# A transformer block kernel: gate and readout pages issued from Pool's queue instead of SyncE's, and gate products spaced out at first

## The chip, the cores and the metric

The kernel runs on one core of a Trainium2 chip. The time is device microseconds of one execution, from the first to the last instruction and what lies around them; the figure given is the median of three executions. The profile is of one further execution, with its own time.

## The reference, cut to what matters

The block computes, for 512 latent tokens of width 2048 (and 256 context tokens that only set the starting state of a recurrence): modulation of the normalised input, one projection to 2048 channels, then two token mixers side by side, a pooling over four window sizes and a complex diagonal state-space scan ("S5") in both directions; an output projection; a gated residual; then a gated feed-forward of width 5632 with a 3x3 depthwise convolution, and a second gated residual.

```python
mx = jnp.split(s_c @ w_ada[l] + b_ada[l], 6, axis=-1)
u_lat = h_lat @ w_in[l]
hl = s5_scan(lat_g, lam_re, lam_im, bb_re, bb_im, h0, rev)
lat_dirs.append(s5_readout(hl, ssm_c_re[l, d], ssm_c_im[l, d]))
mix_lat = mix_project(u_lat, lat_dirs[0] + lat_dirs[1], w_pool[l], pool_scale[l], ssm_d[l], w_glu[l], w_out[l])
x = x + mx[2][:, None, :] * rms_norm(mix_lat, g_post_mix[l])
f_lat = conv_glu_ffn(modulate(rms_norm(x, g_pre_ffn[l]), mx[3], mx[4]), w_up[l], w_conv[l], w_down[l], rows)
x = x + mx[5][:, None, :] * rms_norm(f_lat, g_post_ffn[l])
```

Two of the six parts of `mx` are needed at once and are made by TensorE. The other four (called gates below: `mx[2]`, `mx[3]`, `mx[4]`, `mx[5]`) are needed only later; they are matrix-vector products that VectorE makes in the background, page by page.

## The kernel before, in words

**Weights.** All weights come in pages of 128 x 1024 fp32 (512 KB). `Stream` holds them in the order of use: `load` issues a page's transfer on SyncE's queue (L60, tile `raw`, two buffers), `make` splits it into a high part on ScalarE (L77, `whi`) and a low part on VectorE (L78, `wlo`), and `get` hands both to the caller, making one page ahead. Each product of matrices is three matmuls (`mm3`, L176 to L178: high by high, high by low, low by high), so a page is 24 matmuls of 512 columns.

**Foreground and background.** The foreground is the stream of weight pages: 24 pages of the input projection (`u_block`, tile `ub`), 8 of the pooling weights, 24 of the output projection (`wout_block`, tile `wo`) with the two pages of the gated unit among them (`glu`), 8 more of the output projection for the state-space channels (tile `wq`, weights `wbh` and `wbl`), then the feed-forward's pages (tiles `uh`, `up`, `dn`). Everything else is a generator in `Threads`: at each `tick` the foreground gives the generators a budget (the tick's nominal microseconds times a share: 0.76, later 0.84 and 0.95; one weight page counts 5.2), and they are stepped in order of priority. Each `yield c, lag` charges c to the budget and puts the next step at least `lag` weight pages later. The order in which the program is written out is the order of each engine's queue, and every engine works its queue in order.

**The generators that matter here.** `front` (priority 0) brings the state-space input into place (`UT`, products `bp`), adds `scan` (priority 2, on VectorE), copies the states out (`SN`), and runs the readout. `gemv` (priority 3) makes the gate products: each step issues the transfer of the page after next into the two-buffer tile `gv` (`gvload`, L172, on SyncE's queue) and then multiplies a page on VectorE (L972, `scr<-gv,srow`), at a charge of 1.4 and no lag. There are 82 such products. The gated unit, late in the output projection, needs the first 32 of the 96 gate pages (14 of them are multiplied earlier, outside `gemv`), and the transposes of `norm_pair` need all (`bg.finish(gv_t)`, L1137).

**The readout** runs in eleven rounds of one weight page each. `cl_build(u)` loads `cu` and `du` on SyncE's queue (L790, L792) and makes `cl` with four Pool operations and two on VectorE (L793 to L805). `window` copies `cl` into `R` on ScalarE (L812 to L814), `eb_mm` multiplies, `e_out` brings the result to DRAM on ScalarE's queue (L827 to L829, tensor `e_scratch`), and a round later `mi_load` reads it back in another shape (L834, tile `Mi`, 256 KB) on SyncE's queue, where it waits until the write has landed; `y_mm` uses it a round later still. Round u writes out, in this order: `eb_mm(u)`, `mi_load(u-1)`, `y_mm(u-2)`, then `window(u+1)`, `e_out(u)`, `cl_build(u+2)`.

Pool makes `mi` in the early part (`mi_build`, L562 to L564), `cl` in the readout, and later multiplies by the gate rows in `gate_piece` (L1088) and subtracts in `norm_pair` (L1159). Between the last `mi_build` and the readout it has no instruction but the clearings of `R`.

Of the kernel before, what the change touches and what calls it, by code (L numbers as in the profile page):

```python
# [129 lines left out]
def emit(tc, A, out, xs_dram, dbg=None):  # L130
    nc = tc.nc
    V, S, PO, PE = nc.vector, nc.scalar, nc.gpsimd, nc.tensor
# [7 lines left out]
    e_dram = nc.dram_tensor("e_scratch", (8, 32, 960), F32, kind="Internal").ap()  # L140
# [19 lines left out]
    def pg(name, shape=(1024,), dt=F32, parts=128):  # L160
        return shaped(sb.tile([128, 1024], dt, name=name, tag="pg", bufs=NPG), shape, slice(0, parts))

    def bank(name, cols=512, parts=128):
        t = ps.tile([128, 512], F32, name=name, tag="bank")
        return t[:parts, :cols]
# [1 line left out]
    def cst(name, shape, dt=F32):  # L167
        return sb.tile(shape, dt, name=name, tag=name)

    def gvload(ap, q=None):  # L170
        r = ring.tile([128, 1024], F32, name="gv", tag="gv", bufs=2)
        nc.sync.dma_start(r[:], ap)  # L172
        return r

    def mm3(o, ahi, alo, bhi, blo, start, stop):
# [391 lines left out]
    def mi_build(k, t, tmp):  # L567
        g0 = 4 * k
        m = t.rearrange("p (r g i h) -> p r g i h", r=2, g=4, i=8)
        for _ in cmul_build(m[:, 0], m[:, 1], BB[:, 0, g0:g0 + 4, :], BB[:, 1, g0:g0 + 4, :], PIN, g0, 4, PO, tmp):  # L570
            pass
        return m
# [4 lines left out]
    def mt_half(k, r):  # L577
        if r == 0:
            mts[k] = pg(f"mt{k}", (2, 4, 128))
        tp = bank("mtp")  # L580
        for g in range(4):
            PE.transpose(tp[:, g * 128:(g + 1) * 128], mis[k][:, r, g].rearrange("p i h -> p (i h)"), ident[:])
        S.activation(mts[k][:, r], tp.rearrange("p (g c) -> p g c", g=4), AF.Copy)
# [96 lines left out]
    def front():  # L680
        def mi_next(k):
            if k < 8:
                cm = pb.tile([128, 512], F32, name="cm", tag="cm", bufs=1)
                mis[k] = mi_build(k, pb.tile([128, 1024], F32, name="mi", tag="mi", bufs=1)[:], cm[:])

        for gb in range(4):
# [5 lines left out]
                                        ap=[[768, 8], [6144, 16], [1, 768]]), uc.rearrange("p i c -> p (i c)"))  # L692
        mi_next(NMT)
        yield 0.0, 1.0
        for gb in range(4):
            u = pg(f"UT{gb}", (8, NCH))
            UT[gb] = u
            nc.sync.dma_start(u, bass.AP(tensor=u_dram.tensor, offset=gb * 128 * 768,
                                         ap=[[96, 8], [6144, 16], [768, 8], [1, 96]]))
            yield 0.0, 0.5 if gb < 3 else 0.75  # L700
        for gb in range(4):
            for kk in range(2):
                k = 2 * gb + kk
                g0 = 4 * k
                if k >= NMT:
                    for r in range(2):
                        mt_half(k, r)
                    mi_next(k + 1)
                    yield 0.0, 0.4
                mt = mts.pop(k)  # L710
                for r in range(2):
                    bp = bank("bp", 4 * NCH)
                    for g in range(4):
                        PE.matmul(bp[:, g * NCH:(g + 1) * NCH], mt[:, r, g, :], UT[gb][:, (g0 + g) % 8, :],
                                  start=True, stop=True)
                    bv = bp.rearrange("p (g c) -> p c g", g=4)
                    dst = B[:, :, r, g0:g0 + 4]
                    S.activation(dst[0:64], bv[0:64], AF.Copy)
                    S.activation(dst[64:128, 0:32][:, ::-1], bv[64:128, 0:32], AF.Copy)
                    S.activation(dst[64:128, 32:96][:, ::-1], bv[64:128, 32:96], AF.Copy)  # L720
                yield 0.0, 1.6 if k == NMT else 0.3
# [65 lines left out]
        def cl_build(u):  # L787
            g4 = slice(4 * u, 4 * u + 4)
            cu = pc.tile([128, 2, 4, 16], F32, name="cu", tag="cu", bufs=3)
            nc.sync.dma_start(cu[:], A["ssm_c"][:, :, g4, :])  # L790
            du = pc.tile([128, 16], F32, name="du", tag="du", bufs=3)
            nc.sync.dma_start(du[:], A["ssm_d"][u])  # L792
            PO.tensor_tensor(du[:], du[:], hmask[:], op=OP.mult)  # L793
            cl = [pc.tile([128, 4, 8, 16], F32, name=f"cl{r}", tag=f"cl{r}", bufs=4)[:] for r in range(2)]
            ts = [p1.tile([128, 528], F32, name="cm", tag="ps2", bufs=2)[:, :512].rearrange(
                "p (g s h) -> p g s h", g=4, s=8) for _ in range(2)]
            sh = [128, 4, 8, 16]
            pr, pi = [POUT[:, :, r, g4].rearrange("p s g -> p g s").unsqueeze(3).to_broadcast(sh) for r in range(2)]
            xr, xi = [cu[:, r].unsqueeze(2).to_broadcast(sh) for r in range(2)]
            V.tensor_tensor(ts[0], xi, pi, op=OP.mult)  # L800
            PO.tensor_tensor(cl[0], xr, pr, op=OP.mult)
            V.tensor_tensor(ts[1], xi, pr, op=OP.mult)
            PO.tensor_tensor(cl[1], xr, pi, op=OP.mult)
            PO.tensor_tensor(cl[0], cl[0], ts[0], op=OP.subtract)
            PO.tensor_tensor(cl[1], cl[1], ts[1], op=OP.add)  # L805
            cls[u] = (cl, cu, du)
# [9 lines left out]
        def eb_mm(u):  # L816

            ebs[u] = eb = bank("eb", 240)
            for r in range(2):
                for g in range(4):  # L820
                    c = 512 * r + 16 * (4 * u + g)
                    PE.matmul(eb[32 * g:32 * g + 32], BBt[:, c:c + 32], R[r][:, g].rearrange("p m h -> p (m h)"),
                              start=(r == 0), stop=(r == 1))
# [7 lines left out]

        def mi_load(u):
            Mis[u] = mi = pc.tile([128, 4, 8, 16], F32, name="Mi", tag="Mi", bufs=2)
            nc.sync.dma_start(mi[:].rearrange("p g j h -> p g (j h)"),  # L834
                              bass.AP(tensor=e_dram.tensor, offset=u * 32 * 960,
                                      ap=[[16, 8], [960, 16], [240, 4], [1, 128]]))

        ebs = {}
        cl_build(0)
        cl_build(1)  # L840
        yield 2.8, 2.0
# [3 lines left out]
        for u in range(11):  # L845
            if u < 8:
                eb_mm(u)
            if 1 <= u <= 8:
                mi_load(u - 1)
            if 2 <= u <= 9:  # L850
                y_mm(u - 2)
            if u >= 4 and u % 2 == 0:
                yt_mm(u // 2 - 2)
            yield 0.0, 0.5
            if u < 7:
                window(u + 1)
            if u < 8:
                e_out(u)
            if 2 <= u <= 9:
                y_act(u - 2)  # L860
            if u >= 4 and u % 2 == 0:
                yt_act(u // 2 - 2)
            if u + 2 < 8:
                cl_build(u + 2)
            yield 1.4, 0.5

    yT, yTr = [None] * 2, [None] * 4
# [95 lines left out]
    def gemv():  # L963
        todo = [(c, n, hf) for c in range(3) for n in range(16) for hf in range(2)][2 * NGP:]
        tiles = []
        for x in range(len(todo)):

            while len(tiles) < min(x + 2, len(todo)):
                c, nt, hf = todo[len(tiles)]
                tiles.append(gvload(A["ada_n"][c, nt, hf]))  # L970
            c, nt, hf = todo[x]
            V.scalar_tensor_tensor(scr[:], tiles[x][:], 1.0, srow[:, hf * 1024:(hf + 1) * 1024], op0=OP.mult,  # L972
                                   op1=OP.mult, accum_out=gacc[:, hf, c, nt:nt + 1])
            tiles[x] = None
            gv_state[0] = 2 * NGP + x + 1
            if nt == 15 and hf == 1:
                gfin(c)
            yield 1.4, 0

    def gfin(c):  # L980
        a = acol[:, c, :]
# [123 lines left out]
    def norm_pair(rep):  # L1105
# [33 lines left out]
        for kk in range(8):  # L1139
# [21 lines left out]
            yield 1.8 * (kk % 2), 0  # L1161

    fr_t = bg.add(front(), 0)
    gv_t = bg.add(gemv(), 3)
    pb_t = []
    phs = {}
# [75 lines left out]

    frow = [pg(f"frow{j}", (2, 512)) for j in range(2)]

    def gemv5():
        for hf in range(2):
            sr = p2.tile([128, 1024], F32, name="srow2", tag="srow2", bufs=1)
            nc.sync.dma_start(sr[:], A["c_row"][:, hf * 1024:(hf + 1) * 1024])
            S.activation(sr[:], sr[:], AF.Silu)
            for nt in range(16):  # L1250
                r = gvload(A["ada_n"][3, nt, hf])
                yield 0.0, 1
                V.scalar_tensor_tensor(scr[:], r[:], 1.0, sr[:], op0=OP.mult, op1=OP.mult,
                                       accum_out=gacc[:, hf, 3, nt:nt + 1])
                yield 1.2, 0
        gfin(3)
        yield from rows_of(3, frow, p2, "srow2", 1)
# [134 lines left out]
    r = None  # L1392
    for t in range(4):
        os = {d: bank(f"df{d}") for d in (2, 3)}
        gps = []
        for d in (2, 3):
            for j in range(2):
# [3 lines left out]
                for k in range(2):  # L1401
                    g = gt[NP - GRP + 2 * j + k]
# [16 lines left out]
        r = rows_rstd(st8[:, t:t + 1, :], 0, 4)[0]  # L1419
# [88 lines left out]
```

## Time and profile before

| what | value |
|---|---|
| median of 3 executions | 2184.66 us (2183.29 to 2185.28) |
| the profiled execution's own time | 2184.42 us |
| its span, first to last instruction | 2182.6 us |
| TensorE busy | 2073.6 us |
| mean granted TensorE clock | 0.978 of full speed |

The profiled execution lies 0.24 us under the median and has 1.8 us around its span. PE is TensorE, PEld its weight load, DVE VectorE, ACT ScalarE, POOL GpSimd, SP SyncE; an engine's name with a q is its queue of DMA issues and waits. A row of the timeline gives the start, the length, the engine, the line, the operation, out<-in, and in brackets how long the engine had been idle before and what ended that. A row of the windows gives a stretch, its length, each engine's busy time in it, the granted clock, the share of the DMA engines' time and GB/s.

### The profile page before, as it was taken

What the parts mean: (1) busy time and instruction counts of PE and PEld (TensorE: products, weight loads), DVE (VectorE), ACT (ScalarE), POOL (GpSimd) and SP (SyncE); (2) the same over time, 40 slices, a digit from 0 to 9 for tenths busy, and PEclk for the clock granted to TensorE, in tenths of its full rate; (3) what the DMA queues carried; (4) which work ended last, traced back from release to release, by engine and by line L of the source; (5) the groups of instructions that cost most, each with busy time, mean ns of one, the idle gap of its engine ahead of it and who ended that gap; (6) DMA issues with size and microseconds to landing.
All of it is one profiled execution on the core that took longest, in us unless ns stands there. A gap on an engine that the chain in (4) does not pass through costs nothing.

```text
span 2182.6 us, 24482 instructions
## 1 busy us (share of the span) xinstructions
PE 2073.6 (95%) x9468; PEld 1639.6 (75%) x9468; DVE 1545.1 (71%) x2135; ACT 690.7 (32%) x969; POOL 261.7 (12%) x318
## 2 busy tenths in 40 slices
PE   7997999788798999999999999999999999999996
PEld 3576877566587888888888888888888888888885
DVE  1576899655667688767777777777766767767676
ACT  4343325433256323322222222222222222222224
POOL 5951100262016000000000000000000000000004
PEclk8899999899998999999999999999999999999998
DMA  9877423666656233333333433333322322333225
GB/s 380 302 285 258 167 85 121 211 186 193 211 205 229 68 97 116 118 123 116 123 110 116 135 116 117 125 114 114 102 90 93 97 95 90 96 96 97 90 95 192
DMA packets 94292, 315.00 MB, mean 144 GB/s; under 512 B 16992, under 2 KB 22880, under 8 KB 89952
## 3 DMA queue, kind: packets, MB, share of 16 engines
q1 hardware_dynamic: 90848, 306.07, 42.3%
q10 hardware_dynamic: 3328, 7.37, 0.9%
q8 instruction: 74, 1.21, 0.2%
q14 instruction: 42, 0.34, 0.0%
HBM read 302.46 MB, written 10.94 MB: 144 GB/s over the span
## 4 chain that ended last, share of the span: by engine, by line
PE 74%; DMA 10%; DVE 10%; issue 3%; ACT 3%; POOL 1%; SPq 0%; ACTq 0%; DVEq 0%; POOLq 0%
PE up L176 14%; PE up L178 14%; PE up L177 14%; PE dn L178 7%; PE dn L177 7%; PE dn L176 7%; DMA gv<-in_ada_n 5%; DVE wlo L78 2%; DVE scr L972 2%; DVE sct L664 1%; PE ada L446 1%; DVE B L665 1%; DMA e_scratch<-E 1%; ACT scr L1086 1%; DMA raw<-in_w_up 1%
## 5 line engine op out<-in xcount | busy, mean ns | idle before, releaser
L78 DVE TENSOR_TENSOR wlo<-raw,whi 128x1024 fp32r<-128x1024 f32 (+1 forms) x326 | 407.3, 1250 | 362.8 <-ACT whi L77 359.8
L77 ACT ACTIVATE whi<-raw 128x1024 fp32r<-128x1024 f32 (+1 forms) x326 | 341.4, 1048 | 795.0 <-PE dn L178 313.2
L1274 DVE SCALAR_TENSOR_TENSOR cv<-zp,wconv,cv 128x512 f32<-128x512 f32 x704 | 528.1, 750 | 18.8
L176 PE MATMUL up<-h,whi 128*128 128x512 f32 x1344 | 531.4, 395 | 0.0
L177 PE MATMUL up<-h,whi 128*128 128x512 f32 x1344 | 530.8, 395 | 0.0
L178 PE MATMUL up<-h,wlo 128*128 128x512 f32 x1344 | 530.8, 395 | 0.0
L178 PEld LDWEIGHTS up<-h,wlo 128*128 128x128 f32 x1344 | 251.9, 187 | 61.8
L177 PEld LDWEIGHTS up<-h,whi 128*128 128x128 f32 x1344 | 251.9, 187 | 61.5
L176 PEld LDWEIGHTS up<-h,whi 128*128 128x128 f32 x1344 | 251.9, 187 | 61.4
L178 PE MATMUL dn<-whi,g 128*128 128x512 f32 x672 | 265.5, 395 | 0.0
L176 PE MATMUL dn<-whi,g 128*128 128x512 f32 x672 | 265.5, 395 | 0.0
L177 PE MATMUL dn<-wlo,g 128*128 128x512 f32 x672 | 265.5, 395 | 0.0
L1088 POOL TENSOR_TENSOR facc<-facc,frow 128x512 f32<-128x512 f32 x11 | 15.4, 1423 | 1434.9 <-ACT scr L1086 1434.9
L972 DVE SCALAR_TENSOR_TENSOR scr<-gv,srow 128x1024 bf16<-128x1024 f32 x82 | 114.1, 1392 | 86.6 <-DMA gv<-in_ada_n 86.3
L1308 ACT ACTIVATE zp<-up 128x512 f32<-128x512 f32 x84 | 50.5, 601 | 378.6 <-PE up L178 378.6
L177 PEld LDWEIGHTS dn<-wlo,g 128*128 128x128 f32 x672 | 126.0, 187 | 30.8
L178 PEld LDWEIGHTS dn<-whi,g 128*128 128x128 f32 x672 | 126.0, 187 | 30.8
L176 PEld LDWEIGHTS dn<-whi,g 128*128 128x128 f32 x672 | 126.0, 187 | 30.8
L177 PE MATMUL wo<-wlo,mx 128*128 128x512 f32 x192 | 81.3, 424 | 32.1 <-DVE wlo L78 32.1
L1322 DVE TENSOR_TENSOR facc<-facc,dn 128x512 f32<-128x512 f32 x144 | 92.1, 680 | 0.7 <-PE dn L178 0.7
L178 PE MATMUL ub<-hT,wlo 128*128 128x512 f32 x192 | 77.2, 402 | 11.9 <-DVE wlo L78 11.9
L176 PE MATMUL wo<-whi,mx 128*128 128x512 f32 x192 | 80.5, 419 | 0.0
(276 smaller groups left out, 2441.9 us busy)
## 6 DMA issues: line engine op xcount, KB each, us to landing
raw<-in_w_up SPq DMA_DIRECT2D x176, 512.0 KB, 3.6
gv<-in_ada_n SPq DMA_DIRECT2D x114, 512.0 KB, 4.5
raw<-in_w_down SPq DMA_DIRECT2D x88, 512.0 KB, 3.6
adak<-in_ada_k SPq DMA_DIRECT2D x32, 1024.0 KB, 8.6
raw<-in_w_out SPq DMA_DIRECT2D x32, 512.0 KB, 5.0
raw<-in_w_inp SPq DMA_DIRECT2D x24, 512.0 KB, 4.9
adag<-in_ada_n SPq DMA_DIRECT2D x7, 1024.0 KB, 8.7
xl<-in_xT SPq DMA_DIRECT2D x8, 512.0 KB
```

What stands on the lines that cost most here:

```text
L77: nc.scalar.activation(hi[:, :n], raw[:, :n], AF.Copy)
L78: nc.vector.tensor_tensor(lo[:, :n], raw[:, :n], hi[:, :n].bitcast(F32), op=OP.subtract)
L176: PE.matmul(o, ahi, bhi, start=start, stop=False)
L177: PE.matmul(o, ahi, blo, start=False, stop=False)
L178: PE.matmul(o, alo, bhi, start=False, stop=stop)
L446: PE.matmul(ada[q, w][32 * g:32 * g + 32, :], scol[:, 4 * j + g, :], t[:, g, :], start=j == 0, stop=j == 3)
L664: V.tensor_tensor(tv, y[:, :, r], p[:, sl].unsqueeze(1).to_broadcast([128, n, 2, 32]), op=OP.mult)
L665: V.tensor_tensor(x, x, tv, op=OP.add)
L972: V.scalar_tensor_tensor(scr[:], tiles[x][:], 1.0, srow[:, hf * 1024:(hf + 1) * 1024], op0=OP.mult, op1=OP.mult, accum_out=gacc[:, hf, c, ...
L1274: V.scalar_tensor_tensor(a[:], zz, wcol, a[:], op0=OP.mult, op1=OP.add)
L1308: S.activation(zp[j][i % 2][:, 1:9, 1:65], o.rearrange("p (r c) -> p r c", r=8), AF.Copy)
L1322: V.tensor_tensor(f, f, os[t], op=OP.add)
```

## The change

`gvload` takes its queue from a small shared list. It starts as SyncE's queue with a lag of one weight page for every gate product; from the eighth piece of `front` (`k == 7`) it is Pool's queue with no lag; when the readout begins it is SyncE's queue again, and from the end of the readout's eighth round Pool's. `mi_load` goes to Pool's queue always. The last gate (`gemv5`, in the feed-forward) uses SyncE's queue as before. Nothing that is computed changes.

```diff
+    gv_q = [nc.sync, 1.0]
+
-    def gvload(ap, q=None):
+    def gvload(ap):
         r = ring.tile([128, 1024], F32, name="gv", tag="gv", bufs=2)
-        nc.sync.dma_start(r[:], ap)
+        gv_q[0].dma_start(r[:], ap)
         return r
...
                     mi_next(k + 1)
+                    if k == 7:
+                        gv_q[:] = [nc.gpsimd, 0]
                     yield 0.0, 0.4
...
             Mis[u] = mi = pc.tile([128, 4, 8, 16], F32, name="Mi", tag="Mi", bufs=2)
-            nc.sync.dma_start(mi[:].rearrange("p g j h -> p g (j h)"),
-                              bass.AP(tensor=e_dram.tensor, offset=u * 32 * 960,
+            PO.dma_start(mi[:].rearrange("p g j h -> p g (j h)"),
+                         bass.AP(tensor=e_dram.tensor, offset=u * 32 * 960,
                                       ap=[[16, 8], [960, 16], [240, 4], [1, 128]]))
...
         ebs = {}
+        gv_q[0] = nc.sync
         cl_build(0)
...
                 cl_build(u + 2)
+            if u == 7:
+                gv_q[0] = nc.gpsimd
             yield 1.4, 0.5
...
                 gfin(c)
-            yield 1.4, 0
+            yield 1.4, gv_q[1]
...
     frow = [pg(f"frow{j}", (2, 512)) for j in range(2)]
 
+    gv_q[0] = nc.sync
+
     def gemv5():
```

## Rows read from the trace of the kernel before

**Rows 1.** The page's first part: busy time, share of the span, instructions.

```profile
PE 2073.6 (95%) x9468; PEld 1639.6 (75%) x9468; DVE 1545.1 (71%) x2135; ACT 690.7 (32%) x969; POOL 261.7 (12%) x318
```

**Rows 2.** The windows, all engines: stretch, length, busy, clock, DMA share, GB/s.

```profile
168.00:200.00 32.00, 21.45 (x80) 16.07 (x81) 19.95 (x29) 8.23 (x15) 9.73 (x6) 0.89 0.73 238
...
260.00:366.00 106.00, 101.12 (x429) 79.68 (x428) 101.30 (x191) 35.83 (x53) 0.00 (x0) 1.00 0.28 87
366.00:410.00 44.00, 36.75 (x150) 28.65 (x149) 28.28 (x42) 26.09 (x26) 1.86 (x4) 0.96 0.68 230
...
438.00:514.00 76.00, 65.12 (x416) 47.51 (x415) 45.30 (x56) 31.29 (x59) 46.00 (x30) 0.96 0.61 172
...
541.00:592.00 51.00, 41.68 (x176) 32.32 (x175) 28.36 (x42) 13.04 (x17) 0.00 (x0) 0.94 0.69 234
592.00:637.00 45.00, 41.46 (x189) 34.20 (x188) 31.00 (x53) 20.47 (x31) 5.09 (x4) 0.95 0.64 217
...
700.00:2182.00 1482.00, 1462.40 (x6390) 1180.01 (x6388) 1082.86 (x1426) 400.40 (x504) 32.01 (x25) 1.00 0.34 110
```

**Rows 3.** The timeline of TensorE: rows with idle time before them.

```profile
189.38 0.80 PE L178 MATMUL ub<-hT,wlo 128*128 128x512 f32 x1 [7.56 <-DVE wlo L78]
...
388.24 0.50 PE L177 MATMUL wo<-wlo,mx 128*128 128x512 f32 x1 [2.12 <-DVE wlo L78]
...
420.21 0.79 PE L177 MATMUL wo<-wlo,mx 128*128 128x512 f32 x1 [7.80 <-DVE wlo L78]
```

**Rows 4.** The timeline of VectorE, early.

```profile
186.95 1.23 DVE L972 SCALAR_TENSOR_TENSOR scr<-gv,srow 128x1024 bf16<-128x1024 f32 x1 [6.94 <-DMA gv<-in_ada_n]
...
188.10 1.22 DVE L78 TENSOR_TENSOR wlo<-raw,whi 128x1024 fp32r<-128x1024 f32 x1
```

**Rows 5.** The timeline of VectorE, one weight page of the output projection.

```profile
388.78 1.23 DVE L972 SCALAR_TENSOR_TENSOR scr<-gv,srow 128x1024 bf16<-128x1024 f32 x1 [0.60 <-DMA gv<-in_ada_n]
...
391.42 1.23 DVE L972 SCALAR_TENSOR_TENSOR scr<-gv,srow 128x1024 bf16<-128x1024 f32 x1 [1.40 <-DMA gv<-in_ada_n]
...
395.11 1.22 DVE L78 TENSOR_TENSOR wlo<-raw,whi 128x1024 fp32r<-128x1024 f32 x1
```

**Rows 6.** All instructions on tile gv: nanoseconds min/median/max; waits; landing times.

```profile
L172 SPq DMA_DIRECT2D gv<-in_ada_n x114: 327/328/2359, 169.9 to 1536.8; - x114
...
  DVE scr L972: 86.3, 48
...
DMA to landing us min/median/max: 3.6/4.5/8.9
```

**Rows 7.** The windows of line 972 alone: VectorE busy (two instructions a product).

```profile
168.00:200.00 32.00, 9.08 (x12) 0.89 0.73 238
200.00:260.00 60.00, 19.52 (x28) 1.00 0.65 215
```

**Rows 8.** The waits of SyncE's queue, 410 to 541 us: total, times, longest.

```profile
SPq L834 <- DMA e_scratch<-E: 47.2, 8, 7.8
```

**Rows 9.** The timelines of ScalarE, SyncE's queue and Pool in the readout, by time.

```profile
438.36 0.54 ACTq L829 DMA_DIRECT2D e_scratch<-E  x1
446.36 0.64 SPq L834 DMA_DIRECT2D Mi<-e_scratch  x1
...
447.59 0.57 SPq L790 DMA_DIRECT2D cu<-in_ssm_c  x1
...
453.70 0.58 POOL L793 TENSOR_TENSOR du<-du,hmask 128x16 f32<-128x16 f32 x1 [4.54 <-DMA du<-in_ssm_d]
...
457.81 2.27 POOL L804 TENSOR_TENSOR cl<-cl,cm 128x512 f32<-128x512 f32 x1
...
460.11 0.58 ACT L812 ACTIVATE R<-cl 64x448 f32<-64x448 f32 x1 [7.28 <-POOL cl L804]
...
465.30 0.52 ACTq L829 DMA_DIRECT2D e_scratch<-E  x1
...
514.10 0.52 ACTq L829 DMA_DIRECT2D e_scratch<-E  x1
```

## Prediction: what the change will do

> **What bounds the kernel.** The first part of the page [rows 1] shows TensorE busy in 95% of the span, so time can be won or lost only where it stands idle or runs at the lower clock. The windows [rows 2] say where that is. From 700 us to the end it works 1462.40 of 1482 us, and of the change only the last gate reaches there, whose queue stays as it was. The reader is to look at the stretches between 168 and 700 us: 10.55 us idle of the 32 from 168, 4.9 of the 106 from 260, 7.25 of the 44 from 366, 10.9 of the 76 from 438 (the readout), 9.3 of the 51 from 541, 3.5 of the 45 from 592. The timeline of TensorE [rows 3] then says for what: each larger gap ends with `wlo`, the low half of a weight page, from VectorE. VectorE itself is not full there (19.95 of 32, 28.28 of 44); its own timeline [rows 4, 5] shows that it stands before a gate product whose page has not landed, with the weight page's `wlo` next in its order. The waits for gate pages sum to 86.3 us in 48 pieces [rows 6]. In the readout it is another thing: SyncE's queue stands 47.2 us before the reads of `Mi` [rows 8].
>
> **Spacing the gate products at first.** Before the scan starts 20 products run (40 instructions, two each, in [rows 7]). With a lag of one weight page there is one a page until the eighth piece of `front`. Its pauses up to there sum to 8.5 pages (1.0, then 2.25, six of 0.3 that a quarter-page tick rounds to 0.5, 0.5, 1.75), so nine products, and two follow before the scan takes the whole budget: 11. What goes away is the stall of 7.56 us at 189 us [rows 3]: VectorE waited 6.94 us for a page of the third product and made `wlo` only at 188.10 [rows 4], though its page had long been split. With a page's time between products the gate page is there. Of the 10.55 us idle from 168 us [rows 2], 1.7 belong to ScalarE's work on `mt`; the clock of 0.89 is worth another 2.4 (0.11 of the 21.45 busy). I take 10 us; from below 3, if the crowded transfers (DMA share 0.73) make the next weight page late in place of the gate page; from above 13. From 200 to 260 us TensorE was not idle, so the seven or so products that go from there free nothing. The scan starts about a page sooner, in the stretch where VectorE is busy 101.30 of 106 us [rows 2]: 1 us, of the 4.9 idle.
>
> **The nine products that move.** The output projection still takes three a page (0.84 x 5.2 / 1.4), so the nine come out at the end of the list, in the first pass over the `wq` pages, 592 to 637 us, where before the products ended. They need 9 x 1.23 = 11.1 us of VectorE [rows 5] and, at the mean wait of 86.3/82 = 1.05 us [rows 6], 9.5 us of waiting, 20.6 in all; VectorE has 45 - 31.0 = 14 us free there [rows 2]. The rest, 6.6, is late for `norm_pair`, for which TensorE soon waits. I take a loss of 6; bounds 0 (all in the gaps) and 14 (nothing of the free time can be used, since it lies in waits for ScalarE, less what TensorE's second pass hides).
>
> **Reading `Mi` on Pool's queue.** The chain is in [rows 9]. `E` of round 0 goes out at 438.36; SyncE issues the read of `Mi` 8.0 us later, and only behind it `cu` (447.59) and `du` for the round after next; these land 6.1 us later, Pool starts at 453.70, needs 6.4 us up to its subtraction's end (457.81 + 2.27), ScalarE makes `R` from 460.11, and `E` of round 2 goes out at 465.30. So 26.9 us for two rounds, and over six rounds (438.36 to 514.10) 12.6 us each. Moved, `cu` and `du` no longer stand behind the wait; Pool itself stands before `E`'s landing, issues the read, and goes on with `cl_build`. The 7.34 us from 446.36 to 453.70 leave the chain, and Pool's own issue of 512 short rows comes in. Nothing of before shows it: from below SyncE's 0.64 us [rows 9], from above two of Pool's long operations, 4.5 (2 x 2.27). I take 2. The chain is then 26.9 - 7.3 + 2 = 21.6 for two rounds, 10.8 a round. TensorE needs 65.12/76 x 12.6 = 10.8 us a round too, some of it at the lower clock. I take 11 a round, since `y_mm`, the weights and the products still disturb each other: 6 x 1.6 = 10 us won (bounds 4 and 14). What is queued behind the new wait is Pool's `cl_build`, and ScalarE waits for that, with `whi` behind it on ScalarE.
>
> **The start of the readout.** `cu` and `du` of rounds 0 and 1 stand behind gate pages on SyncE's queue; in this stretch gate pages are on Pool's queue, and the gap of 7.80 us at 420 us [rows 3] begins with VectorE and Pool waiting for `cu` and each other. I take 4 us won (0 to 8).
>
> **Gate pages through Pool's queue.** In the output projection the gate products set the pace: 388.78 and 391.42 are 2.64 us apart, three of them and `wlo` at 395.11 make a page some 8 us long [rows 5], and TensorE waits over 2 us in each (2.12 at 388 [rows 3]). With two buffers, a page's transfer starts when the product before last is done, so the spacing is half of (landing + product): (4.2 + 1.3)/2 = 2.75, with 4.2 between the least (3.6) and the median (4.5) of [rows 6]. SyncE's other loads don't hold these up, so leaving its queue wins nothing here; what counts is how much later a page lands when Pool issues it. Each product then costs half of that: 14 products before the readout and 21 from its end to the `wq` pages, less three that TensorE's lead of a page covers, so 16 us for each us of delay. The trace has no transfer issued by Pool. From below: no queue behind weight pages, landing in 3.6, that is -0.6 us or -10. From above: a Pool operation of 2.27 us in place of SyncE's 0.33 [rows 6, 9], +1.9 or +30. The nearest row is Pool's own short instruction, 0.58 us, against 0.33, and the 128 rows of a page must be described too; I take +0.6, a loss of 10.
>
> The Trainium skill has a price for it (DMA: Bandwidth & Descriptors, Anatomy of one DMA, SWDGE path): about 2.0 us and the bytes at 436 GB/s for a transfer issued by Pool, which for 512 KB is an estimate of 3.2 us. By it this term would be a gain of 16 us and the time about 2149; by the rows as I read them it is a loss of 10. The same page (Latency and other measured facts) gives the first byte as about 1 us from Pool against 0.6 from SyncE, which would make it a loss of 6. No row here shows a transfer of Pool's.
>
> **Sum.** 2184.42 (the profiled execution, 0.24 under the median) - 10 - 1 + 6 - 10 - 4 + 10 = 2175.4, so 2175 us, 0.4% under.
>
> **Rivals.** *Pool's transfers are slow.* If a gate page lands later by more than 16 x d = 10 + 9, d = 1.2 us, the change loses. At +1.7 the term is 27 and the time 2192. For it: Pool's operations beside VectorE's take up to 2.27 us; against it: Pool is idle in those stretches (0.00 from 541 [rows 2]). Chance 0.15. The Trainium skill has a rule that speaks this way (SBUF — State Buffer, SBUF: two separate sides): Pool cannot write the descriptors of its transfers while VectorE runs in a mode that takes both ports, as plain copies and products with a scalar may. By it the delay would fall where VectorE makes `dg`, not where it makes products.
>
> *The wait only changes place.* Pool stands before `E` and issues slowly, so `cl`, `R` and `whi` come as late as before: the readout and its start win nothing, 2184.42 - 11 + 6 + 10 = 2189. It decides where the readout and its start win less than the 5 us that the other terms lose: from an issue of some 5 us ((19.6 + 5)/2 = 12.3 a round). Chance 0.07.
>
> *The terms cancel:* early stall only half gone (-5), moved products at 10, the rest as above: 2184.42 - 5 - 1 + 10 - 10 - 4 + 10 = 2184. Chance 0.15.
>
> *Pool's transfers are no slower.* The Trainium skill's rule that transfers run on the same engines whichever queue issued them (DMA: Bandwidth & Descriptors, Issuing engines are not separate DMA queues) would lead there. The term is 0 to -10 and the time 2165 to 2155; I put it at 2162. For it: the gate page no longer stands in a line with the weight pages. Chance 0.23.
>
> **How the numbers follow.** The forecast, 2167 to 2180, has 0.40, which with 0.23 is faster by over 0.2% (4.4 us, about what three executions of this kernel, 2 us apart, can tell): 0.63. Within it: 0.15. Slower: 0.22. For 8 in 10 the range leaves out the upper half of the slow-Pool case and the end of the other: 2156 to 2192.
>
> **What would show it.** TensorE's gap at 189 us gone, and nine products fewer before the scan; 11 us from one `E` to the next; SyncE's wait for `e_scratch` gone and one on Pool in its place; products in the output projection a little over 3 us apart; products among the `wq` pages up to the last before the second pass. It is wrong if products on Pool's queue are 2.7 us apart or less (too slow a forecast) or over 3.3 (too fast), or if `cl` waits on Pool's own issue.

## The result, and the profile after

The changed kernel takes 2201.26 us (median of four, 2198.99 to 2204.95), the kernel before in the same runs 2184.95 us: a ratio of 1.0078, interval 1.006 to 1.0095. So it is slower by some 17 us, where 2175 was forecast. The profiled execution took 2202.6 us with a span of 2200.8.

The windows of the kernel after answer to [rows 2] (stretch, length, busy time of the engines in the order TensorE, its weight loads, VectorE, ScalarE, Pool, then clock, DMA share, GB/s):

```profile
168.00:200.00 32.00, 30.38 (x145) 24.27 (x146) 22.55 (x30) 13.07 (x28) 11.65 (x6) 1.00 0.70 220
...
366.00:410.00 44.00, 33.90 (x123) 25.93 (x121) 24.87 (x36) 21.13 (x23) 15.72 (x22) 0.88 0.64 212
438.00:514.00 76.00, 63.97 (x394) 49.06 (x395) 49.62 (x54) 33.95 (x64) 45.74 (x35) 0.89 0.64 188
541.00:592.00 51.00, 38.17 (x145) 29.04 (x143) 29.37 (x44) 12.33 (x15) 7.93 (x15) 0.90 0.66 226
592.00:637.00 45.00, 37.45 (x156) 30.11 (x157) 30.45 (x51) 16.67 (x27) 10.34 (x13) 0.89 0.70 234
637.00:700.00 63.00, 45.41 (x199) 38.31 (x198) 45.72 (x84) 31.44 (x66) 24.58 (x26) 0.79 0.45 163
700.00:2182.00 1482.00, 1478.24 (x6521) 1195.51 (x6519) 1082.55 (x1425) 410.35 (x518) 34.30 (x32) 1.00 0.35 111
```

The window from 637 us was not among the rows of before. There it reads, in the kernel before:

```profile
637.00:700.00 63.00, 54.72 (x314) 47.89 (x313) 50.63 (x89) 44.67 (x88) 31.12 (x33) 0.86 0.51 184
```

The reader sees both halves of the story at once. The first window has what was forecast: TensorE at work for 30.38 of 32 us instead of 21.45, at full clock. The last one before 700 us has what was not: 45.41 us in place of 54.72, at 0.79.

Windows shift when work moves, so the better measure is when a given weight page is split on VectorE (`wlo` or `wbl`, line 78): it comes in the same order in every kernel. The table gives, from one profile each, how much later (+) or earlier (−) than in the kernel before each stretch between such pages was passed, in us; the runs of single parts stand beside the change and are told below. Programs that do not differ before the first `wo` page still reach it 2 us apart or so (the five with the change's own start: −9.9 to −6.0), so a single entry is good to about 2 us.

| stretch, by page (its start in the kernel before) | after | pace_only | gates_pool_only | mi_pool_only | no_pace |
|---|---|---|---|---|---|
| up to the first `wo` page (362.2) | −8.3 | −6.2 | +1.7 | −0.8 | +3.2 |
| to the seventh `wo` page (403.8) | +5.9 | +2.0 | +3.0 | −0.5 | +3.3 |
| to the 19th `wo` page (536.8), over the readout | −3.8 | −1.6 | −1.1 | −3.3 | −6.0 |
| to the first page of `wq` (596.1) | +2.0 | −2.9 | +1.2 | −0.4 | −1.2 |
| to the third `uh` page (677.4) | +20.5 | +10.5 | +0.4 | +0.5 | −0.5 |
| together | +16.3 | +1.8 | +5.2 | −4.5 | −1.2 |

From there to the last weight page nothing more changes but 0.6 us at most. So one stretch decides, that of the moved products: 20.5 us lost, where the prediction had 6. (The expectations call the page at its end the second `uh` page.)

Line 979 makes the products now. Its windows answer to [rows 7], two instructions a product: 22 instead of 40, 11 products before the scan, as counted out beforehand.

```profile
168.00:200.00 32.00, 5.70 (x6) 1.00 0.70 220
200.00:260.00 60.00, 9.83 (x16) 1.00 0.49 165
```

The tile `gv`, after [rows 6]: issues on Pool (nanoseconds min/median/max), VectorE's waits for a page (us, times), and landing. The landing row holds only transfers whose landing the trace knows, here Pool's.

```profile
L174 POOL DMA_DIRECT2D gv<-in_ada_n x51: 527/528/785, 231.9 to 649.6; - x51
...
  DVE scr L979: 84.4, 43
...
DMA to landing us min/median/max: 3.7/4.1/8.4
```

SyncE's waits from 410 to 541 us, after [rows 8]: the wait for `E` is gone from this queue, and another has grown.

```profile
SPq L174 <- DVE scr L979: 68.8, 17, 8.6
```

### The profile page after: what moved, and what is told of

Read it like the earlier page. It is cut to its first block, busy times and chain, and to the rows that moved or that the text cites. A ratio compares the mean times of both kernels' runs of the same rounds, so it can differ in the third digit from the quotient of the medians.

```text
span 2200.8 us, 24510 instructions
## 1 busy us (share of the span) xinstructions
PE 2083.1 (95%) x9468; PEld 1649.3 (75%) x9468; DVE 1557.5 (71%) x2135; ACT 690.8 (31%) x969; POOL 298.5 (14%) x377
## 4 chain that ended last, share of the span: by engine, by line
PE 65%; DVE 2%; ACT 1%; DMA 1%; issue 1%; POOL 0%; DVEq 0%; ACTq 0%; SPq 0%; POOLq 0%
PE up L178 14%; PE up L179 14%; PE up L180 14%; PE dn L180 7%; PE dn L178 7%; PE dn L179 7%; ACT scr L1093 1%; PE uh L179 0%; PE uh L180 0%; PE uh L178 0%; DMA raw<-in_w_up 0%; DMA raw<-in_w_down 0%; DVE facc L1095 0%; DMA rawb<-in_w_up 0%; DVE wlo L78 0%
## 5 line engine op out<-in xcount | busy, mean ns | idle before, releaser
L1095 POOL TENSOR_TENSOR facc<-facc,frow 128x512 f32<-128x512 f32 x11 | 15.4, 1419 | 1435.0 <-ACT scr L1093 1435.0
```

Source lines behind the costliest of these rows:

```text
L1095: eng.tensor_tensor(m, m, row[d // 2][:, d % 2, :], op=OP.mult)
```

## Experiments

Each run was made beside runs of the kernel before; a ratio below 1 is faster, and 0.001 is 2.2 us.

**One part at a time.** *Spacing alone*: the changed kernel with every queue it switches set to SyncE's, `Mi`'s too.

```
-                        gv_q[:] = [nc.gpsimd, 0]
+                        gv_q[:] = [nc.sync, 0]
...
-            PO.dma_start(mi[:].rearrange(...
+            nc.sync.dma_start(mi[:].rearrange(...
...
-                gv_q[0] = nc.gpsimd
+                gv_q[0] = nc.sync
```

> Only the spacing of the gate products at first; all transfers on SyncE's queue as before. Both theories: the stall of 7.56 us at 189 us is gone and the first page of the output projection comes 8 to 10 us sooner. Theory 'late products': the nine products that then fall among the wq pages and behind them hold norm_pair back whatever queue their pages come through, some 17 us from the wq pages to the first page of the feed-forward, so 2190 to 2194 us. Theory 'Pool's transfers': the same nine cost about 6 us on SyncE's queue, as predicted, and the rest of the late loss is Pool's landing and its gate products standing behind transfers, so 2179 to 2183 us.

2184.86 us, 1.0001 (0.9993 to 1.001): nothing, and between the two theories. The table says why: 6 us won early, 10.5 lost with the nine products, small gains and losses between.

*Gate pages through Pool alone*: the changed kernel with `gv_q = [nc.sync, 0]` at first and `Mi` on SyncE's queue.

> Only the gate pages through Pool's queue in the two stretches; no spacing, Mi read on SyncE's queue. Both theories: the pages of the output projection before the readout lose 7 us, the start of the readout wins 4. Theory 'late products': nothing is lost behind the wq pages, so 2188 to 2196 us with what the second stretch loses. Theory 'Pool's transfers': another 10 us are lost among the wq pages and in norm_pair, so 2196 to 2206 us.

2190.15 us, 1.0027 (1.0015 to 1.0039): 6 us lost, about half of what was forecast.

*Reads of `Mi` alone*: the kernel before with one line changed.

```
-            nc.sync.dma_start(mi[:].rearrange(...
+            PO.dma_start(mi[:].rearrange(...
```

> Only the read of Mi on Pool's queue. Theory 'chain': one E comes after another in 11.8 us instead of 12.6 and nothing is lost after the readout, 2178 to 2182 us. Theory 'the wait changes place': Mi is read later than before because Pool's cl_build stands ahead of it, y_mm waits for it, and the readout as a whole wins less than 2 us, 2183 to 2187 us.

2180.56 us, 0.9987 (0.9977 to 0.9997): some 3 us won.

*All but the spacing*: the changed kernel with `gv_q = [nc.sync, 0]` at first.

> The changed kernel without the spacing: gate pages through Pool in the two stretches and Mi on Pool. Theory 'late products': 9 us lost early and some 17 won behind the wq pages against the changed kernel's 2201, so 2191 to 2196 us. Theory 'Pool's transfers': the early stall comes back and only 6 us are won late, so 2202 to 2206 us.

2186.81 us, 1.0013 (1.0003 to 1.0022), less than either theory had. Spacing alone costs nothing, the two queue changes together under 3 us, all three 17 us. The parts are not additive: some 14 us arise only where spaced products meet Pool's queue. By the table 10.5 us of this lie behind the first `wq` page (20.5 against 10.5 and −0.5) and 6 just before it (+2.0 against −2.9 and −1.2).

**What the late loss is.** `norm_pair(0)` begins on VectorE with four `xin` operations (line 1123, before it 1116). Their start against that of the kernel before, and the start of the third `uh` page against its 677.4:

| kernel | `xin` starts | against 645.16 | page |
|---|---|---|---|
| mi_pool_only | 640.65 | −4.5 | −4.5 |
| no_pace | 643.95 | −1.2 | −1.2 |
| pace_only | 646.97 | +1.8 | +1.8 |
| half_pace | 647.58 | +2.4 | +2.4 |
| gates_pool_only | 650.39 | +5.2 | +5.2 |
| sync_back | 653.29 | +8.1 | +8.1 |
| mult_late | 660.56 | +15.4 | +15.4 |
| after | 661.49 | +16.3 | +16.3 |

To the tenth of a microsecond these kernels are as late as `norm_pair`. What VectorE does ahead of it sets the time; TensorE's second pass over the `wq` pages, which was thought to cover part of it, covers nothing: in the kernel after it ends 7.79 us before TensorE can go on. Two rows of TensorE's timeline in the kernel after show it standing still for it:

```profile
656.17 0.80 PE L178 MATMUL wq<-wbh,mx 128*128 128x512 f32 x1 [3.46 <-DVE macc L1092]
...
671.22 5.84 PE L1154 MATMUL h2p<-ident,macc 128*128 128x128 f32 x28 [7.79 <-DVE macc L1092]
```

(Each row is a group of instructions, with its idle time before it.) And VectorE stands before gate pages, with Pool's timeline beside it:

```profile
641.01 1.23 DVE L979 SCALAR_TENSOR_TENSOR scr<-gv,srow 128x1024 bf16<-128x1024 f32 x1 [2.97 <-DMA gv<-in_ada_n]
...
653.45 1.23 DVE L979 SCALAR_TENSOR_TENSOR scr<-gv,srow 128x1024 bf16<-128x1024 f32 x1 [4.91 <-DMA gv<-in_ada_n]
```

```profile
633.43 3.53 POOL L1095 TENSOR_TENSOR macc<-macc,bb 128x512 f32<-128x512 f32 x2 [4.83 <-ACT scr L1093]
636.90 1.12 POOL L174 DMA_DIRECT2D gv<-in_ada_n  x2
...
646.16 3.53 POOL L1095 TENSOR_TENSOR macc<-macc,pio 128x512 f32<-128x512 f32 x2 [3.08 <-ACT scr L1093]
649.63 0.58 POOL L174 DMA_DIRECT2D gv<-in_ada_n  x1
```

The buffer for the page of 636.90 was free at 630.79, when the product before last ended. Pool was then standing before ScalarE's `scr` (4.83 us), with its own multiplication behind that and the page's issue last. So four issues came 5.1, 6.1, 1.7 and 6.1 us after their buffers were free; the others, without Pool's work ahead, 0.3 us.

**Pool's queue taken out there.** The changed kernel, with the gate pages back on SyncE's queue for the `wq` pages:

```
     bg.share = 0.95
+    gv_q[0] = nc.sync
```

> The whole change, but from the wq pages on the gate pages go through SyncE's queue again. Theory that the second 10 us of the late loss come from Pool's queue (by its line behind Pool's gate multiplications or by the later landing): the loss between the first wq page and the second uh page falls from 20.5 us to about 10, the time from 2201 to 2190 us. Rival, that the products themselves and their delay from the output projection make it: the loss stays at 17 us or more and the time at 2198 or more.

2189.09 us, 1.0023 (1.0013 to 1.0034). The loss in that stretch is 10.8 us (−2.7 to +8.1, from a profile 5 us slower than the median run), as with spacing alone. The second 10 us are Pool's queue; by the times it is 12.

What each half is made of shows in VectorE's busy time from the first `wq` page to the start of `norm_pair` (stretch, length, busy, clock, DMA share, GB/s): the kernel before, pace_only, the kernel after, sync_back.

```profile
596.09:645.16 49.07, 33.24 (x61) 0.97 0.60 204
...
587.37:646.97 59.60, 43.52 (x78) 0.94 0.68 238
...
591.85:661.49 69.64, 43.54 (x78) 0.90 0.58 196
...
593.43:653.29 59.86, 43.27 (x78) 0.97 0.66 228
```

With spacing alone 14 products fall in it instead of 6. VectorE is busy 10.3 us longer, and idle 16.1 us against 15.8: the added products took none of its idle time. In the kernel after it is as busy as that but idle for 26.1 us, and nearly all the difference is waits for gate pages: 14.5 us instead of 5.3 (5.0 in sync_back).

**Is it the line or the landing?** *Multiplications on VectorE* in the first pass, then in both:

```
-            yield from gate_piece(..., V if d == 3 or (rep == 1 and d >= 3) else PO)
+            yield from gate_piece(..., V if rep == 0 or d == 3 else PO)
```

> The whole change, but the multiplications by the gate row in the first half of the wq pages run on VectorE instead of Pool, so Pool's queue holds nothing before the gate pages' issues there. Theory that the line behind these multiplications on Pool's queue makes the second 10 us: the loss between the first wq page and the second uh page falls from 20.5 to some 12 us (10 and the six multiplications on VectorE), the time to 2192. Rival, that it is the later landing through Pool's queue: the loss stays at 18 us or more, the time at 2199 or more.

2199.8 us, 1.0065 (1.0052 to 1.0078). `norm_pair` began 14.5 us earlier than in the kernel after (646.97), and nothing was won: the scheduler charges VectorE's multiplications, so the last two products fell behind `norm_pair`, and the last page stood behind four multiplications of the second pass on Pool:

```profile
657.45 5.92 POOL L1095 TENSOR_TENSOR macc<-macc,bb 128x512 f32<-128x512 f32 x4 [16.83 <-ACT scr L1093]
663.32 0.59 POOL L174 DMA_DIRECT2D gv<-in_ada_n  x1
```

VectorE waited for it until 668.91, 7.86 us, and `h2` needs the columns that this product ends.

> The whole change with all multiplications by the gate row on VectorE, in the second pass over the wq pages too, so that nothing of Pool's stands ahead of the gate pages' issues there. With only the first pass's moved, norm_pair began some 14 us earlier, but the last gate page's issue then stood behind four of the second pass's on Pool (5.92 us). Theory that the line behind Pool's own work makes the second 10 us of the late loss: the loss between the first wq page and the second uh page falls from 20.5 to some 12 us, the time to about 2192. Rival, that the later landing through Pool's queue makes it: the loss stays at 18 us or more and the time at 2198 or more.

(The second run: `V` for every piece.) 2201.37 us, 1.0081 (1.0067 to 1.0094). Now no issue stands behind Pool's work, but VectorE, the engine that sets the time here, has ten more multiplications ahead of the last product, each behind a wait of some 0.85 us for ScalarE, and makes that product at 665.82. Both runs change order and load as well as the line, so neither answers the question.

*Multiplications later*, with queue, engine and order of the products kept: the six of the first pass are issued together after the last gate page's issue.

```
-        eng.tensor_tensor(m, m, row[d // 2][:, d % 2, :], op=OP.mult)
+        if eng is None:
+            late.append((m, row[d // 2][:, d % 2, :]))
...
+        if d == 3:
+            for m, r in late:
+                PO.tensor_tensor(m, m, r, op=OP.mult)
...
```

> The whole change, with Pool's six multiplications by the gate row in the first pass over the wq pages issued together after the last gate page's issue instead of between the issues; queue, engine and order of the products stay. In the changed kernel four issues stood 5.1, 6.1, 1.7 and 6.1 us behind these, and VectorE's waits after them sum to 9.7 us. Theory that the line makes the second 10 us: the loss between the first wq page and the second uh page falls from 20.5 to some 12 us and the time to about 2192. Rival, that the later landing through Pool's queue makes it: the loss stays at 18 us or more and the time at 2198 or more.

2200.05 us, 1.0063 (1.0048 to 1.0078), as the rival had it; the loss in the stretch is 17.4 us (−2.0 to +15.4) instead of 20.5. Every issue now follows its buffer by 0.3 us, and pages land late in place of being issued late:

```profile
635.08 0.53 POOL L174 DMA_DIRECT2D gv<-in_ada_n  x1 [4.76 <-DMA gv<-in_ada_n]
637.36 0.53 POOL L174 DMA_DIRECT2D gv<-in_ada_n  x1 [1.75 <-DVE scr L979]
```

```profile
642.70 1.23 DVE L979 SCALAR_TENSOR_TENSOR scr<-gv,srow 128x1024 bf16<-128x1024 f32 x1 [5.64 <-DMA gv<-in_ada_n]
```

They landed 7.5 and 7.7 us after issue. VectorE's waits for gate pages in this stretch sum to 14.5 us after, 11.1 here, and 5.0 with SyncE's queue (sync_back). So taking the line away wins some 3 us of these waits, and 6 stay with Pool's queue and no line. In time the run can't be told from the kernel after: the late multiplications also slow three small operations of VectorE's just ahead of `norm_pair`, by 3 us in all (last section), and one profile of each carries the split. On SyncE's queue a gate page waited for was used 3.9 to 6.4 us after issue in the same crowd (DMA share 0.86 from 628 to 645 us, here 0.79): there it stands ahead of the weight pages and `x` rows that SyncE issues after it, while on Pool's queue it lands later beside them. That it shares the engines with them is how I read these rows; no run took them away.

**How much spacing.** *Half a page* between products, all queues SyncE's (`gv_q = [nc.sync, 0.5]`), and the same with `Mi` on Pool's:

> The first gate products stand half a weight page apart instead of a whole one, and every load stays on SyncE's queue: 16 products before the scan (20 before the change, 11 with a whole page), so five fewer to place late. Theory that the late loss goes by the number of products that run past the first wq pages: with a whole page it was 10.5 us for nine, with four it is under 4 us and the early gain stays 6 to 8 us, 2177 to 2181 us in all. Rival, that the early gain needs the whole page: the stall of TensorE near 189 us is back and the time is 2183 to 2186.

> Half a page between the first products and the reads of Mi on Pool's queue; the gate pages stay on SyncE's. Theory that these two terms are independent once the late loss is small: 6 to 8 us from the early stretch, 4 from the readout, under 4 late, 2173 to 2178 us. Rival, that they disturb each other as spacing and Pool's queue did in the whole change: 2181 us or more.

2186.59 us, 1.0005 (0.9997 to 1.0014), and 2186.06 us, 1.0006 (0.9997 to 1.0015). The late loss was as small as the first theory had it (−0.8 to +2.4, 3.2 us for four products), but the early gain was gone: +4.3 at the first `wo` page. The third and fourth products wait again, with the weight page behind them:

```profile
188.53 1.23 DVE L979 SCALAR_TENSOR_TENSOR scr<-gv,srow 128x1024 bf16<-128x1024 f32 x1 [4.76 <-DMA gv<-in_ada_n]
...
194.02 1.23 DVE L979 SCALAR_TENSOR_TENSOR scr<-gv,srow 128x1024 bf16<-128x1024 f32 x1 [4.26 <-DMA gv<-in_ada_n]
```

TensorE then works 23.56 of the 32 us from 168, at a clock of 0.82: little more than before, and slower.

*A whole page, but only up to the last `UT` load*, `Mi` on Pool's queue, gate pages on SyncE's:

```
+            if gb == 3:
+                gv_q[1] = 0
```

> A whole page between products only up to the last load of UT, none from there on, so 16 products before the scan instead of 11; Mi on Pool's queue, gate pages on SyncE's. Theory that the early gain comes from the crowded stretch up to 200 us alone and the late loss from the number of products left: 6 to 8 us early, 4 in the readout, 3 to 4 lost late, 2176 us. Rival, that the stall comes back once the spacing ends, as with half a page: the first wo page no earlier than before, 2183 us or more.

2180.52 us, 0.9977 (0.9969 to 0.9986): no more than `Mi`'s move alone. The stall of 189 us was gone (−8.9 us there), yet by 260.6 us the kernel was level with before: TensorE waits 2.61 us at 211 for a weight page behind three products with waits of 4.22, 1.27 and 1.72 us. A gain at one place in a stretch is not yet one at its end.

**The readout.** If what cost there was `cu` and `du` standing behind the wait for `E` [rows 9], loading them a round earlier must win it without touching `Mi`'s queue:

```
+        def cu_load(u):
+            cu = pc.tile(..., bufs=4)     # and du; as in cl_build before
...
         def cl_build(u):
+            cu, du = cus.pop(u)
...
             if u + 2 < 8:
+                if u + 3 < 8:
+                    cu_load(u + 3)
                 cl_build(u + 2)
```

> The kernel before with one thing changed: cu and du of the readout are loaded one round earlier, on SyncE's queue as before, and Mi too stays there. Theory of the prediction's step on Mi, that what costs is cu and du standing behind the wait for E: a round falls from 12.6 to 11 us or less, 8 to 10 us won, 2175 us. Rival, that Mi's own landing and the products hold the round: the round stays above 12 us and the time at 2181 or more.

> As the run before it, and the reads of Mi on Pool's queue. Theory that with Mi on Pool's queue cu and du were still late, since they stood behind SyncE's waits for gate products: 4 to 6 us more than Mi's move alone (2180.6), 2175 us. Rival, that Mi's landing sets the round once it is on Pool's queue: 2180 us, no more than Mi's move alone.

The earlier load alone: 2177.77 us, 0.9966 (0.9954 to 0.9978), the fastest kernel of the study, 7 us under before. SyncE still stands 49.5 us before the reads of `Mi` from 410 to 541 us, so the wait itself was not the price. But a round takes 11.8 us (441.69 to 512.46), not 11, and no less than with `Mi` moved alone (11.7, 436.90 to 507.35). Over the readout 2.6 us are won, and 4.2 from there to the first `wq` page; why they are won there stays open. With `Mi` on Pool's queue as well: 2182.48 us, 0.9986 (0.9977 to 0.9995), so Pool's queue takes some 4 us back. Nothing is won over `Mi`'s move alone (2180.56), so there it is not `cu` and `du` that hold the round: the rival stands. With `Mi` moved alone SyncE's queue was no freer; from 410 to 541 us it stood before the buffers of gate products instead (34.3 us in the kernel before):

```profile
SPq L172 <- DVE scr L972: 79.5, 21, 11.3
```

and Pool issues `Mi` behind its own `cl_build`, in the kernel after:

```profile
436.23 2.24 POOL L808 TENSOR_TENSOR cl<-cl,cm 128x512 f32<-128x512 f32 x1
438.44 2.24 POOL L809 TENSOR_TENSOR cl<-cl,cm 128x512 f32<-128x512 f32 x1
440.62 1.12 POOL L838 DMA_DIRECT2D Mi<-e_scratch  x1
```

`E` of that round went out at 430.28; its read was issued 10.3 us later, against 8.0 on SyncE's queue in [rows 9]; over the eight rounds the mean is 8.5 against 5.4.

*Spacing and the earlier load together* (pace_only with `cu_load`):

> The spacing of the change with every load on SyncE's queue, and cu and du loaded a round earlier. Theory that the two act in different stretches and add: spacing alone was 0, the earlier load alone -7, together 2178. Rival, that a shorter readout leaves the scheduler fewer pages for products, so that more of them end up among the wq pages: 2183 or more.

2182.82 us, 0.9992 (0.9984 to 1.0): 2 us where 7 were expected. Up to the first `wq` page they do add: 12.8 us ahead, the furthest of all kernels, against 8.7 and 5.0 alone. Then the nine products take their price again, 10.7 us to the third `uh` page, as in pace_only. By the pages 2.1 us are left, by the single runs 1.8 − 5.4 = −3.6, which the table cannot tell apart; why the times are further apart than the pages I cannot say.

## Why the prediction was wrong

**Early spacing: right, and somewhat smaller.** 10 + 1 us were forecast; the kernel after reaches the first `wo` page 8.3 us earlier, other kernels with the same start 6.0 to 9.9. The gap of 7.56 us at 189 us is gone, and the products before the scan are 11, as the tally had it. What the runs add is that it needs the whole page all through `front`.

**The nine products: the step that failed.** The prediction let them use 14 us of VectorE's free time in 592 to 637 us, and charged what was left, 6. Alone, on SyncE's queue, they cost 10.5, close to their bare 11.1 us of work. From the first `wq` page to `norm_pair` VectorE has eight products more, is busy 10.3 us longer and idle just as long (16.1 us, 15.8 before): its free time lies in waits for ScalarE, 12.1 of the 15.8 us before, and the products took none of it. Waits for gate pages grew by only 2 us there, where the prediction had 9.5. That is nearly the case the prediction bounded at 14 and set aside. `norm_pair`'s start sets the end of the stretch one to one.

**Two terms were added that are not independent.** The cost of Pool's queue was worked out from landings in the output projection, with Pool idle, and for 35 products; that the moved nine would also go through it, in the stretch where Pool makes gate multiplications and stands before ScalarE for them, entered neither term. [Rows 2] had Pool at work there (5.09 us from 592) and idle only up to it. Pool's queue added 10 us to the nine, nearly all of it waits for gate pages: some 3 went with the line, the rest stayed without it. Together 20.5 us stand against the 6 of the sum.

**Gate pages through Pool: right in sign, too large in size.** 10 us forecast, 6 measured alone, most of it at the two places named. From the third `wo` page to the seventh 13 products take 39.5 us in the kernel after, 3.04 each, against 12 in 32.2 us, 2.68, before: "a little over 3 us" holds there, and behind the readout they are 2.9 apart. A landing of 4.1 us (median) against the 4.2 assumed for SyncE's queue would have cost nothing by the formula (and [rows 6] give landings for only 13 of 114 pages, four of them the last gate's), so the median hides what counts: 11 of the 51 pages on Pool's queue landed after more than 5.5 us, where without spacing (no_pace, gates_pool_only) it was 3 of 42 each. The page issued while VectorE made `dg` (603.59) landed after 4.8 us, so of the delay that the first rival placed there no more than 0.7 shows.

A weight page issued 0.9 to 1.0 us behind does not make a gate page late by itself. Of 13 such gate pages seven landed after 3.8 to 4.2 us; the gate page ahead of them had landed or had at most 1.15 us left. Six landed after 6.3 to 7.3 us; with five of these the one ahead had 2.0 us or more left, with the sixth it isn't known. The other runs part in the same way, but for the page of 7.5 us in mult_late. And where the five kernels with the change's own start still have one program, from the 19th `wo` page to the first `wq` page, gate_vector_all, with one landing over 5.5 us, lost 0.0 us and the others, with two to five, 2.0 to 4.0. So pages close behind each other on Pool's queue, beside a weight page, are slow; that spacing brings them close is how I read it, no run tests it.

The Trainium skill (DMA: Bandwidth & Descriptors, Anatomy of one DMA, SWDGE path) gave 3.2 us, an estimate from its figures; the least here is 3.7, and 3.2 without the 0.53 of the issue. The Trainium skill's rule on queues (the same page, Issuing engines are not separate DMA queues) fits the crowded landings, but did not make Pool's pages as fast as SyncE's.

**`Mi` on Pool's queue: half the chain.** Forecast 10 us and 4 at the start; measured 3 alone. Rounds are 11.8 us (430.28 to 501.10), not 11. Taking `cu` and `du` from behind the wait, by either way, wins 0.8 us a round (12.6 to 11.8) instead of 1.6, so they were not all that held it. Moving `Mi` left them behind the products' waits on the same queue, and put `Mi` behind `cl_build` on Pool; loading them earlier as well won nothing more. The rival in which the wait only changes place described part of this, though it named Pool's slow issue (1.02 to 1.12 us here) and not Pool's own work ahead of it. At the start the gap of 7.80 us is 6.14 with the gate pages' move alone and 3.45 in the kernel after.

**Sum, by the single runs:** 0 + 6 − 3 = 3 us, where 2175.4 − 2184.42 = −9 was forecast. The other 14 are the products that meet Pool's queue. What stays open: why a page on Pool's queue lands late where others are under way, why cu_early wins the larger part of its 7 us behind the readout, and why spacing and the earlier load of `cu` and `du` give less time together than apart.

## What to carry to other kernels

Work that a scheduler puts off comes out where the list ends; ask which wait ends there, and count it in full if the engine that does it also starts the next stage. Before moving transfers to an engine's queue, follow that queue to the last transfer, and look for waits of the engine's own, not its busy share: an idle engine that stands before another holds the queue all the same. And when loads are late behind a wait, loading them earlier won more here (7 us) than moving the wait (3), though not where it was expected.

## What the runs showed of the hardware

Pool issues a page of 128 rows in 0.53 us and the 512 short rows of `Mi` in 1.02 to 1.25 us, against 0.33 and 0.64 on SyncE's queue. A 512 KB page issued by Pool lands after 3.7 us at the least and 4.1 at the median, and with a weight page issued by SyncE 0.9 to 1.0 us behind it after 3.8 to 4.2 us or after 6.3 to 7.3, by how far the gate page ahead was from landing (1.15 us at most, 2.0 at least); 7.5 and 7.7 in the densest stretch. Pool's multiplication of 128x512 elements took 1.25 to 2.29 us. While three of them ran, three small operations of VectorE's on 128x16 elements took 1.13 to 1.19 us instead of 0.17 (mult_late, 650.81 to 654.38), and each ended 0.03 us after one of the three (651.91, 653.13, 654.35).
